# A two-layer fp32 encoder on one core: casts tied behind the last activation, operand sums by kind, residual loads tied to the stream

## The chip, the cores and the metric

The kernel runs on one core of one Trainium2 chip. The metric is the device time of one execution in microseconds (us). TensorE (PE) multiplies, ScalarE (ACT) casts and activates, VectorE (DVE) adds, subtracts and splits, GpSimd (POOL) and SyncE (SP) mostly start DMA transfers, each on a queue of its own: SP's is the hardware queue (q1), POOL's the software queue (q0).

## The reference

The encoder has two layers over 1024 tokens of width 1024, each with a mixer and a gated feed-forward part, with a layer norm behind each sum:

```python
for layer in range(DEPTH):                      # DEPTH = 2
    y = even_mixer(...) if layer % 2 == 0 else odd_mixer(...)
    x = layer_norm(DN_ALPHA * x + y, mix_ln_g[layer], mix_ln_b[layer])
    x = layer_norm(DN_ALPHA * x + swiglu(x, ffn_w_gate[layer], ffn_w_up[layer], ffn_w_down[layer]),
                   ffn_ln_g[layer], ffn_ln_b[layer])

def swiglu(x, w_gate, w_up, w_down):
    return (jax.nn.silu(x @ w_gate) * (x @ w_up)) @ w_down
```

The even mixer is latent attention with a Fourier branch, the odd one a gated unit whose spatial part mixes positions inside blocks of 128; each ends in an output projection. Everything is float32.

## The kernel before

An fp32 product is made of three matmuls. `split` makes of a tile a high part (ACT cast, line 135: `xoh`, `whi`) and a low part (DVE subtraction, line 136: `xol`, `wlo`), and `mm3` multiplies high by high (line 141), high by low (142) and low by high (143). So TensorE can't begin with a page before its cast, nor go past the first matmul before its subtraction.

After the even front (to about 557 us) the kernel is a row of stages: the output projection of the mixer (called mix), feed-forward part 0 (ffn0), the spatial part of the odd layer, its projection (odd), and feed-forward part 1 (ffn1). Each projection and each down-projection is a **reduce**.

A reduce works in seven products in place of eight (half-size blocks, with sums of blocks made before), in the order p = 1, 5, 6, 4, 7, 2, 3. A product runs over groups g of two page pairs. `load(p, g)` calls `stream`, which has SP fetch 512 KB of H (left pages, or their sums SA and SB) and 512 KB of W (right pages, or their sums TA and TB) into one of six `rx` tiles and splits them into one of six pairs of cells; a group is 24 matmuls of 128x512. The stage before has its last pages stored to memory by POOL, and the sums of the last page pairs (`page_sums`, lines 317 to 320) stored behind it, and the first groups of the next reduce (`lead`) are already loaded while it runs.

Besides, the reduce adds the residual: eight tiles of 512 KB, `xt[half, s]`, loaded by POOL (line 463), in all but the mix reduce multiplied by a gain and given a bias by `gained` (DVE, lines 469 and 470), then joined with the result from PSUM by `add` (line 457). The tiles come from pools that the stage before still uses, so a residual load waits for the tile's last reader. The two loads of the last mix page pair (`job`) and the stores of its sums go through POOL too.

The normalised rows are transposed and become operands of the following feed-forward part: besides four plain blocks, the sums S1 (made before) and, per slot s of four, S2, S4 and S3 (`all_sums`); each is a DVE subtraction (line 131) and a split. The feed-forward part's first two units, which run interleaved, take plain blocks first, then S2, S4 and S3. A unit ends in `emit`: a DVE addition (kept as `last_v`) and a Silu on ACT.

The order on each engine is made by a scheduler from the program's order, dependences and estimated readiness. `behind(marks)` adds an edge: an instruction is not put before the marked one on the same engine. `marks` are the instructions of the last `stream`: SP's DMA, ACT's cast, DVE's subtraction.

Of the kernel before, what the change touches and what calls it, by code (L numbers as in the profile page):

```python
# [112 lines left out]
class Trunk:  # L113
# [109 lines left out]
    def run(self):  # L223
        tc, nc, a = self.tc, self.nc, self.a
        with ExitStack() as top:
# [24 lines left out]
            self.vd = D_("vd", [P, NT, 256], 8)  # L250
            self.ahead = None
            with ExitStack() as fs:
# [156 lines left out]
    def reduce(self, st, resid, rgb, ln, keep, pre=None, left=()):  # L409
# [30 lines left out]
        def load(p, g):  # L440
            if (p, g) not in ops:
                ops[p, g] = self.stream(st, p, groups[g], raws, pairs)

# [16 lines left out]

        def residual(half):
            for s in range(4):
                nc.gpsimd.dma_start(xt[half, s], resid[token(half, s)])

# [44 lines left out]

        def sums(s):  # L510
            (a11, a12), (a21, s1) = kept[0, s], kept[1, s]
            self.sub(s1, s1, a11)
            self.split(*self.operand(self.S2, s), s1)
            self.sub(a12, a12, s1)
            self.split(*self.operand(self.S4, s), a12)
            self.sub(a21, a11, a21)
            self.split(*self.operand(self.S3, s), a21)

# [6 lines left out]
        def spread(jobs, k, of):  # L525
            i0, i1 = len(jobs) * k // of, len(jobs) * (k + 1) // of
            for j in jobs[i0:i1]:
                j()
        slots = range(4)
        for p in (1, 5, 6, 4, 7, 2):  # L530
            for g in range(n):
                load(p, g)
                if p == 1 and g == 1:
                    load(1, 2)
                    if rgb is not None:
                        rg, rb = (self.bcast(tmp(), a["ln_" + x][rgb[0], rgb[1]]) for x in "gb")
                    residual(0)
                    last = self.job(st, M - 1, True) if st is self.stage["mix"] else None
                if p == 5 and g == 0:
                    residual(1)  # L540
                if p == 6 and g == 0 and keep is None:
                    fg, fb = (self.bcast(self.raw_tile(), a["ln_" + x][ln[0], ln[1]]) for x in "gb")
                if p == 4 and g == 0 and pre is not None:
                    with self.behind(*self.marks):
                        pre()
                if p in (1, 5) and g > 1:
                    spread([lambda s=s: gained(p == 5, s) for s in slots], g - 2, n - 2)
                if p == 2:
                    spread([lambda s=s: normed1(s) for s in slots], g, n)
                for s in slots:  # L550
                    mm(p, g, s)
                    if p == 1 and s % 2 == 1 and left:
                        left.pop(0)()
                    if g == n - 1:
                        if p == 1:
                            add(0, s, lo, p, True)
                        elif p == 5:
                            add(0, s, hi, p, True)
                            add(1, s, hi, p, True)
                        elif p == 6:  # L560
                            add(0, s, hi, p)
                        elif p == 4:
                            add(1, s, lo, p, True, ALU.subtract)
                        elif p == 7:
                            add(1, s, lo, p)
                            add(1, s, hi, p)
                        else:
                            add(0, s, lo, p)
                            stat(0, s, 0)
# [20 lines left out]
        def all_sums():  # L590
            with self.behind(self.late):
                for s in slots:
                    sums(s)
        return [lambda q=q: turn0(q) for q in range(2)], all_sums
# [103 lines left out]
    def ffn(self, w0, weights, st, pend):  # L698
# [4 lines left out]
        def unit(j, w, tiles="yy"):  # L703
            sg = {}

            def emit(half, col, ps, sb, op):
                if col == 0:
                    self.last_v = nc.vector.tensor_tensor(sb, ps, sb, op=op).ins  # L708
                    nc.scalar.activation(sb, sb, AF.Silu)
                    sg[half] = sb  # L710
                    return
# [697 lines left out]
```

## Time and profile before

| | |
|---|---|
| median of 3 runs | 2541.53 us (2537.37 to 2542.77) |
| profiled execution | 2541.83 us |
| its span in the profile | 2540.0 us |
| PE busy | 2456.4 us, 97% |
| DVE busy | 1808.9 us, 71% |
| ACT busy | 1111.1 us, 44% |
| DMA | 170 GB/s over the span |

Busy time is the time in which an engine works on instructions, the span runs from the first to the last instruction, and the execution's time holds something around it. The profile's times in the text count from the start of the span. A row of busy time by stretches has the stretch, its length, then busy us (and instructions) of PE, its weight loads, DVE, ACT and POOL, then the granted clock, the DMA engines' busy share, and GB/s. A row in order of time has start, duration, engine, line, operation, output and inputs, and in brackets the idle time before and what ended it. A row of waits has who waited for whom, the total in us, how often, and the longest.

### The profile page before, as it was taken

Reading aid. Unit: us, or ns where it says so; the run is one execution under the profiler, and the core shown is the slowest. Engines: PE = TensorE matmul, PEld = TensorE weight load, DVE = VectorE, ACT = ScalarE, POOL = GpSimd, SP = SyncE. Lnnn points to the kernel's source line nnn. Section 1 sums busy time; section 2 is a strip of 40 time slices with the busy share of each in tenths; the row PEclk is TensorE's granted clock in tenths of the full one; section 3 lists DMA queues with packets and bytes.
Section 4 is the critical chain, followed back from the end, with each engine's and each line's share of the span. In section 5 each row is a group of like instructions: output and inputs, shape, how many; then the busy total and the mean of one; then the engine's idle time right before and its main releaser. Section 6 shows DMA issues by size and latency. Waiting matters only on the chain.

```text
span 2540.0 us, 33155 instructions
## 1 busy us (share of the span) xinstructions
PE 2456.4 (97%) x12294; PEld 2073.4 (82%) x12294; DVE 1808.9 (71%) x2537; ACT 1111.1 (44%) x1711; POOL 318.5 (13%) x527
## 2 busy tenths in 40 slices
PE   8989999998999999999999999988989999999997
PEld 6778888887878888887889998877878888887885
DVE  4348878767886776768678776768777676677667
ACT  3235555544553333333456446653463333333331
POOL 1000111010111111110002132430011111111001
PEclk9999999998999999999999999999999999999998
DMA  4122333138334444467654554667624444549553
GB/s 175 43 89 71 130 110 125 57 138 282 138 118 174 169 168 162 168 252 251 226 182 172 202 203 137 195 244 276 224 73 163 177 166 155 177 164 329 190 188 140
DMA packets 164329, 431.95 MB, mean 170 GB/s; under 512 B 20136, under 2 KB 26952, under 8 KB 164168
## 3 DMA queue, kind: packets, MB, share of 16 engines
q1 hardware_dynamic: 108216, 232.11, 27.8%
q0 software_dynamic: 55952, 197.73, 20.9%
q8 instruction: 96, 1.57, 0.2%
q14 instruction: 65, 0.53, 0.1%
HBM read 286.64 MB, written 138.41 MB: 167 GB/s over the span
## 4 chain that ended last, share of the span: by engine, by line
PE 81%; DVE 6%; issue 5%; DMA 4%; ACT 2%; POOL 1%; SPq 1%; DVEq 0%; ACTq 0%; POOLq 0%
PE b L142 18%; PE b L141 18%; PE b L143 18%; PE S L1316 6%; PE b L912 5%; PE mm L141 4%; PE mm L142 4%; PE mm L143 4%; PE mm L1335 2%; DVE xol L136 1%; DMA rx<-h 1%; PE b L848 1%; DMA x<-xs 1%; ACT xoh L135 1%; DVE st L475 1%
## 5 line engine op out<-in xcount | busy, mean ns | idle before, releaser
L135 ACT CAST whi<-raw 128x1024 fp32r<-128x1024 f32 (+3 forms) x277 | 261.2, 951 | 383.4 <-PE b L142 240.2
L135 ACT CAST xoh<-rx 128x1024 fp32r<-128x1024 f32 (+1 forms) x252 | 244.5, 1011 | 413.5 <-PE b L142 308.8
L141 PE MATMUL b<-xoh,whi 128*128 128x512 f32 x1040 | 410.7, 396 | 7.9 <-ACT xoh L135 7.9
L136 DVE TENSOR_TENSOR wlo<-raw,whi 128x1024 fp32r<-128x1024 f32 (+3 forms) x277 | 303.4, 1099 | 159.3 <-ACT whi L135 157.1
L142 PE MATMUL b<-xol,whi 128*128 128x512 f32 x1040 | 406.8, 391 | 0.0
L143 PE MATMUL b<-xoh,wlo 128*128 128x512 f32 x1040 | 406.4, 391 | 0.0
L136 DVE TENSOR_TENSOR xol<-rx,xoh 128x1024 fp32r<-128x1024 f32 (+1 forms) x252 | 287.6, 1168 | 166.0 <-ACT xoh L135 160.3
L142 PE MATMUL b<-xol,xoh 128*128 128x512 f32 x960 | 379.4, 395 | 22.3 <-DVE xol L136 22.3
L141 PE MATMUL b<-xoh 128*128 128x512 f32 x960 | 376.1, 394 | 8.5 <-ACT xoh L135 8.5
L143 PE MATMUL b<-xoh,xol 128*128 128x512 f32 x960 | 377.5, 393 | 0.0
L141 PEld LDWEIGHTS b<-xoh,whi 128*128 128x128 f32 x1040 | 196.6, 189 | 50.3 <-ACT xoh L135 8.8
L142 PEld LDWEIGHTS b<-xol,xoh 128*128 128x128 f32 x960 | 183.1, 191 | 63.3 <-DVE xol L136 25.5
L143 PEld LDWEIGHTS b<-xoh,wlo 128*128 128x128 f32 x1040 | 196.3, 189 | 41.3
L142 PEld LDWEIGHTS b<-xol,whi 128*128 128x128 f32 x1040 | 196.5, 189 | 40.4 <-issue 0.5
L141 PEld LDWEIGHTS b<-xoh 128*128 128x128 f32 x960 | 182.9, 190 | 47.6 <-ACT xoh L135 9.3
L143 PEld LDWEIGHTS b<-xoh,xol 128*128 128x128 f32 x960 | 183.1, 191 | 38.2
L663 ACT COPY y<-b 128x512 f32<-128x512 f32 x200 | 116.6, 585 | 192.7 <-PE b L143 186.1
L141 PE MATMUL b<-xah,whi 128*128 128x512 f32 x416 | 162.5, 391 | 1.3 <-ACT xah L135 1.3
L142 PE MATMUL b<-xal,whi 128*128 128x512 f32 x416 | 162.0, 389 | 0.0
L143 PE MATMUL b<-xah,wlo 128*128 128x512 f32 x416 | 161.9, 389 | 0.0
L131 DVE TENSOR_TENSOR raw<-raw,raw 128x512 f32<-128x512 f32 (+1 forms) x174 | 128.5, 739 | 28.2 <-DMA raw<-w_up 24.7
L708 DVE TENSOR_TENSOR y<-b,y 128x512 f32<-128x512 f32 x84 | 58.0, 690 | 82.9 <-PE b L143 82.6
(378 smaller groups left out, 4590.9 us busy)
## 6 DMA issues: line engine op xcount, KB each, us to landing
raw<-w_gate SPq DMA_DIRECT2D x44, 512.0 KB, 3.6
raw<-w_up SPq DMA_DIRECT2D x44, 512.0 KB
q<-w_down POOLq DMA_DIRECT2D x44, 512.0 KB, 5.3
h<-x POOLq DMA_DIRECT2D x44, 512.0 KB, 3.7
rx<-h SPq DMA_DIRECT2D x60, 256.0 KB, 3.0
rx<-w_down SPq DMA_DIRECT2D x60, 256.0 KB, 4.3
raw<-o_v SPq DMA_DIRECT2D x16, 512.0 KB, 6.1
x<-o_out POOLq DMA_DIRECT2D x16, 512.0 KB, 5.7
```

The source lines that it names most:

```text
L131: self.nc.vector.tensor_tensor(out, a, b, op=ALU.subtract)
L135: a = self.nc.scalar.copy(hi, src)
L136: return a.ins, self.nc.vector.tensor_tensor(lo, src, hi.bitcast(F32), op=ALU.subtract).ins
L141: mm(ps, lh, rh, start=start, stop=False, skip_group_check=skip)
L142: mm(ps, lh, rl, start=False, stop=False, skip_group_check=skip)
L143: mm(ps, ll, rh, start=False, stop=stop, skip_group_check=skip)
L475: nc.vector.bn_stats(stats[half, s][:, c, :], xt[half, s][:, c * 512:(c + 1) * 512])
L663: nc.scalar.copy(t, ps)
L708: self.last_v = nc.vector.tensor_tensor(sb, ps, sb, op=op).ins
L912: nc.tensor.matmul(ps[:, i * 256:(i + 1) * 256], l[:, b, k, c], r[:, k, :], start=start and k == 0 and i == 0 and m == 0, stop=k == 3 and ...
L1316: nc.tensor.matmul(sc[:, kb, :], l[:, s], r[:, kb * 512:(kb + 1) * 512], start=i == 0, stop=i == 4)
L1335: nc.tensor.transpose(ps[:, k, :], p[:, kt * P:(kt + 1) * P], self.ident)
```

## The change

Four edits, and no change in what is computed. Behind the first edited lines of the changed program line numbers are higher by up to nine.

1. `emit` also keeps the last Silu as `last_a` (the spatial part its last Gelu, by the same attribute). In a reduce, the casts and subtractions of product 1's groups that are not yet loaded are put behind `last_a` on ACT and `last_v` on DVE. In the mix reduce there is no such mark.
2. A residual tile is loaded by tile, not by half. Ahead of each load stands a memset of one column, and it is put behind the subtraction of the stream's last split. Half 0 goes with groups 1 and 2 of product 1, half 1 with product 1's last group and product 5's first.
3. The gains are spread to one group later for half 0, and from product 5's second group for half 1; the first `add` of half 0 goes from the end of product 1 to product 5's second group.
4. The sums are made by kind, four S2, four S4, four S3, and no longer slot by slot.

```diff
         def load(p, g):
             if (p, g) not in ops:
-                ops[p, g] = self.stream(st, p, groups[g], raws, pairs)
+                with self.behind(*((self.last_a, self.last_v) if p == 1 and self.last_a is not None else ())):
+                    ops[p, g] = self.stream(st, p, groups[g], raws, pairs)
...
-        def residual(half):
-            for s in range(4):
-                nc.gpsimd.dma_start(xt[half, s], resid[token(half, s)])
+        def residual(half, s):
+
+            with self.behind(self.marks[2]):
+                nc.vector.memset(xt[half, s][:, 0:1], 0.0)
+            nc.gpsimd.dma_start(xt[half, s], resid[token(half, s)])
...
-        def sums(s):
+        def sum_of(o, s):
             (a11, a12), (a21, s1) = kept[0, s], kept[1, s]
-            self.sub(s1, s1, a11)
-            self.split(*self.operand(self.S2, s), s1)
-            self.sub(a12, a12, s1)
-            self.split(*self.operand(self.S4, s), a12)
-            self.sub(a21, a11, a21)
-            self.split(*self.operand(self.S3, s), a21)
+            out, a, b = {self.S2: (s1, s1, a11), self.S4: (a12, a12, s1), self.S3: (a21, a11, a21)}[o]
+            self.sub(out, a, b)
+            self.split(*self.operand(o, s), out)
...
-                    residual(0)
                     last = self.job(st, M - 1, True) if st is self.stage["mix"] else None
-                if p == 5 and g == 0:
-                    residual(1)
+                if p == 1 and 0 < g < 3:
+                    for s in (2 * g - 2, 2 * g - 1):
+                        residual(0, s)
+                if (p == 1 and g == n - 1) or (p == 5 and g == 0):
+                    for s in (0, 1) if p == 1 else (2, 3):
+                        residual(1, s)
...
-                if p in (1, 5) and g > 1:
-                    spread([lambda s=s: gained(p == 5, s) for s in slots], g - 2, n - 2)
+                if p == 1 and g > 1:
+                    spread([lambda s=s: gained(0, s) for s in slots], g - 2, n - 1)
+                if p == 5 and g == 0:
+                    spread([lambda s=s: gained(0, s) for s in slots], n - 2, n - 1)
+                if p == 5 and g > 0:
+                    spread([lambda s=s: gained(1, s) for s in slots], g - 1, n - 1)
+                if (p, g) == (5, 1):
+                    for s in slots:
+                        add(0, s, lo, 1, True)
...
-                for s in slots:
-                    sums(s)
+                for o in (self.S2, self.S4, self.S3):
+                    for s in slots:
+                        sum_of(o, s)
...
                     self.last_v = nc.vector.tensor_tensor(sb, ps, sb, op=op).ins
-                    nc.scalar.activation(sb, sb, AF.Silu)
+                    self.last_a = nc.scalar.activation(sb, sb, AF.Silu).ins
```

Three places of the instruction order follow.

TensorE in the mix reduce, where product 5's last groups and product 6's first meet, of before (`b_5626` to `b_5647` are the banks of product 6, `b_5738` to `b_5752` those of product 5's third group, `xoh` and `xol` the split pages):

```order
L141 MATMUL b_5626<-xoh 128x512
L141 MATMUL b_5738<-xoh 128x512
L142 MATMUL b_5738<-xol,xoh 128x512
L141 MATMUL b_5745<-xoh 128x512
L142 MATMUL b_5745<-xol,xoh 128x512
```

and of the change, where the third group's banks are `b_5742` to `b_5756`:

```order
L142 MATMUL b_5640<-xol,xoh 128x512
L143 MATMUL b_5640<-xoh,xol 128x512
L141 MATMUL b_5647<-xoh 128x512
L141 MATMUL b_5742<-xoh 128x512
L142 MATMUL b_5742<-xol,xoh 128x512
L141 MATMUL b_5749<-xoh 128x512
```

Before, one matmul of product 6 stands ahead of product 5's third group; of the change 19 do (six for each of three banks, and one). On POOL's queue of the same place the loads of the page job (`raw<-mix`) moved ahead of all eight residual loads, and the stores of its sums, which stood behind them before as well, are now issued directly behind them, while the loads themselves are later.

VectorE at the start of ffn0's reduce, of before (`rx` tiles are the stream's pages, lines 317 to 320 the last page sums, `gb` gain or bias):

```order
L317 TENSOR_TENSOR x_9736<-x_9550,x_9715 128x512
L318 TENSOR_TENSOR x_9735<-x_9550 128x512
L319 TENSOR_TENSOR x_9735<-x_9736,x_9550 128x512
L469 TENSOR_TENSOR q_9756<-q_9756,gb_9785 128x1024
L320 TENSOR_TENSOR x_9736<-x_9715,x_9735 128x512
L470 TENSOR_TENSOR q_9756<-q_9756,gb_9787 128x1024
L469 TENSOR_TENSOR x_9755<-x_9755,gb_9785 128x1024
L136 TENSOR_TENSOR xol<-rx_9879,xoh 128x1024
L470 TENSOR_TENSOR x_9755<-x_9755,gb_9787 128x1024
L136 TENSOR_TENSOR xol<-rx_9884,xoh 128x1024
```

and of the change:

```order
L320 TENSOR_TENSOR x_9744<-x_9723,x_9743 128x512
L136 TENSOR_TENSOR xol<-rx_9788,xoh 128x1024
L465 MEMSET x_9763 128x1
L465 MEMSET q_9764 128x1
L465 MEMSET q_9765 128x1
L465 MEMSET y_9766 128x1
L136 TENSOR_TENSOR xol<-rx_9853,xoh 128x1024
L136 TENSOR_TENSOR xol<-rx_9858,xoh 128x1024
L136 TENSOR_TENSOR xol<-rx_9889,xoh 128x1024
L136 TENSOR_TENSOR xol<-rx_9894,xoh 128x1024
L472 TENSOR_TENSOR x_9763<-x_9763,gb_9793 128x1024
L472 TENSOR_TENSOR q_9764<-q_9764,gb_9793 128x1024
```

The four memsets come behind the third group's splits, and the splits of two more groups stand between them and the first gain, which before stood ahead of the third group's. On POOL's queue the last page and its two sums moved ahead of the residual loads. ffn1's reduce reads the same.

VectorE at the end of the operand sums of ffn0 (S2, S4 and S3 formed at line 131 and split at line 136; `q_6677` is the last slot's S4), of before:

```order
L131 TENSOR_TENSOR q_6677<-q_6677,x_6479 128x4x128
L131 TENSOR_TENSOR x_6479<-q_6676,x_6479 128x512
L136 TENSOR_TENSOR wlo_6782<-raw_5993,whi_6781 128x1024
L136 TENSOR_TENSOR xol<-q_6677,xoh 128x4x128
L136 TENSOR_TENSOR xol<-x_6479,xoh 128x4x128
```

and of the change, where it is `q_6685`:

```order
L131 TENSOR_TENSOR q_6685<-q_6685,x_6487 128x4x128
L131 TENSOR_TENSOR y_6415<-x_6621,y_6415 128x512
L131 TENSOR_TENSOR x_6439<-x_6621,x_6439 128x512
L136 TENSOR_TENSOR xol<-q_6685,xoh 128x4x128
L136 TENSOR_TENSOR xol<-y_6415,xoh 128x4x128
L136 TENSOR_TENSOR xol<-x_6439,xoh 128x4x128
L131 TENSOR_TENSOR x_6463<-q_6684,x_6463 128x512
L131 TENSOR_TENSOR x_6487<-q_6684,x_6487 128x512
L136 TENSOR_TENSOR wlo_6790<-raw_6001,whi_6789 128x1024
L136 TENSOR_TENSOR xol<-x_6463,xoh 128x4x128
L136 TENSOR_TENSOR xol<-x_6487,xoh 128x4x128
```

Of the 24 instructions of the sums three stand behind the last S4's subtraction before, and nine of the change.

In the odd part, all of the last spatial unit's ACT work and its normalising additions on VectorE now stand ahead of the casts and splits of the odd reduce's third group. In F's place, where that reduce goes from product 1 to product 5, lines 317 to 320 of its last page sums and gains still stand between the pages' splits; the adds of half 0 now stand behind the splits.

## Rows read from the trace of the kernel before

**Rows 1.** The page, part 1: busy time of each engine, share, instructions.
```profile
PE 2456.4 (97%) x12294; PEld 2073.4 (82%) x12294; DVE 1808.9 (71%) x2537; ACT 1111.1 (44%) x1711; POOL 318.5 (13%) x527
```

**Rows 2.** Waits of TensorE, whole span.
```profile
PE b L142 <- DVE xol L136: 22.3, 8, 6.6
...
PE b L141 <- ACT xoh L135: 16.4, 4, 5.0
...
PE b L848 <- ACT whi L839: 8.9, 1, 8.9
```

**Rows 3.** Busy time by stretches of 16 us: eight borders, then two undisturbed ones.
```profile
564.00:580.00 16.00, 12.01 (x42) 9.04 (x41) 4.27 (x4) 4.72 (x5) 2.40 (x5) 0.79 1.04 400
590.00:606.00 16.00, 11.04 (x40) 8.62 (x39) 8.51 (x11) 3.63 (x4) 0.00 (x0) 0.79 0.81 270
714.00:730.00 16.00, 12.26 (x42) 9.20 (x41) 15.90 (x25) 9.44 (x16) 0.00 (x0) 0.79 0.11 34
1138.00:1154.00 16.00, 10.33 (x37) 8.02 (x36) 11.36 (x12) 3.33 (x4) 1.93 (x4) 0.79 1.01 382
1690.00:1706.00 16.00, 7.07 (x29) 5.77 (x28) 8.19 (x10) 9.99 (x19) 2.55 (x4) 0.68 1.04 390
1726.00:1742.00 16.00, 9.45 (x36) 7.38 (x35) 15.90 (x18) 2.37 (x3) 2.14 (x4) 0.79 0.74 269
1896.00:1912.00 16.00, 11.81 (x40) 8.79 (x39) 15.04 (x23) 8.57 (x15) 0.00 (x0) 0.79 0.10 33
2320.00:2336.00 16.00, 10.82 (x39) 8.41 (x38) 12.63 (x12) 3.34 (x5) 1.59 (x3) 0.79 1.02 394
610.00:626.00 16.00, 16.00 (x73) 13.23 (x72) 14.31 (x17) 9.39 (x10) 0.00 (x0) 1.00 0.70 236
740.00:756.00 16.00, 16.00 (x72) 13.27 (x71) 12.72 (x19) 6.54 (x9) 2.13 (x4) 1.00 0.46 165
```

**Rows 4.** Busy time by stretches, ffn0's reduce, a short stall.
```profile
1223.00:1226.00 3.00, 2.06 (x10) 1.38 (x9) 3.00 (x4) 1.83 (x2) 0.00 (x0) 1.00 0.72 210
```

**Rows 5.** Waits of all engines, 564 to 575 us, start of the mix reduce.
```profile
ACT xoh L135 <- DMA rx<-mix: 9.8, 1, 9.8
...
PE b L141 <- ACT xoh L135: 3.5, 1, 3.5
```

**Rows 6.** DMA, 1133 to 1143 us: packets, MB, share by queue; issues, us to landing.
```profile
q0 software_dynamic: 783, 2.87, 70.5%
q1 hardware_dynamic: 701, 1.27, 33.0%
...
x<-xs POOLq DMA_DIRECT2D x3, 512.0 KB, 9.3
```

**Rows 7.** Waits of all engines, 1138 to 1150 us, start of ffn0's reduce.
```profile
PE b L142 <- DVE xol L136: 5.7, 1, 5.7
DVE x L469 <- DMA x<-xs: 4.6, 1, 4.6
```

**Rows 8.** VectorE in order of time, 1700 to 1740 us.
```profile
1721.81 1.22 DVE L469 TENSOR_TENSOR q<-q,gb 128x1024 f32<-128x1024 f32 x1
...
1726.10 0.69 DVE L317 TENSOR_TENSOR x<-x,x 128x512 f32<-128x512 f32 x1 [1.93 <-DMA tp<-x]
...
1734.30 5.77 DVE L136 TENSOR_TENSOR xol<-rx,xoh 128x1024 fp32r<-128x1024 f32 x5
```

**Rows 9.** Groups of instructions by line, VectorE: busy us, mean ns, idle before.
```profile
L1322 DVE RECIPROCAL den<-den 128x1 f32<-128x1 f32 x64 | 10.4, 162 | 16.9 <-ACT p L1321 16.5
```

**Rows 10.** Waits of all engines, 1686 to 1706 us, start of the odd reduce.
```profile
ACT xoh L135 <- DMA rx<-tp: 7.9, 2, 6.4
```

**Rows 11.** VectorE in order of time, 706 to 724 us, the sums of ffn0.
```profile
708.70 0.69 DVE L131 TENSOR_TENSOR y<-y,x 128x512 f32<-128x512 f32 x1
...
720.75 0.68 DVE L131 TENSOR_TENSOR q<-q,x 128x512 f32<-128x512 f32 x1
```

**Rows 12.** Waits of TensorE, 714 to 724 us, start of ffn0.
```profile
PE b L141 <- ACT xoh L135: 3.7, 1, 3.7
```

More of the change, by code (lines that the diff above doesn't have):

```diff
@@ L250, in run @@
             self.vd = D_("vd", [P, NT, 256], 8)
-            self.ahead = None
+            self.ahead = self.last_a = None
             with ExitStack() as fs:
@@ L554, in reduce @@
                     if g == n - 1:
-                        if p == 1:
-                            add(0, s, lo, p, True)
-                        elif p == 5:
+                        if p == 5:
                             add(0, s, hi, p, True)
@@ L566, in reduce @@
                             add(1, s, hi, p)
-                        else:
+                        elif p == 2:
                             add(0, s, lo, p)
```

## The prediction

> **What bounds the kernel now.** I read the page first, then the waits of each engine, then busy time by stretches, then the waits and the order of time at the places that stood out. The span is 2540.0 us, and TensorE is busy for 97% of it, VectorE for 71% [rows 1], so an edit pays only where it takes idle time or half-clock time from TensorE. The profiled execution took 2541.83 us: 1.8 us lie outside the span, and the median of the three runs shown is 2541.53, so I add and subtract from 2541.8 and treat it as the median.
>
> TensorE's waits are few: 22.3 us for the low halves of the left pages in eight waits, 16.4 us for the high halves in four, 8.9 us once for a weight split of the spatial stage [rows 2]. Each is at a border between two stages. An idle stretch is not all it costs: the granted clock falls to 1.2 GHz behind it. The reader sees it best by counting matmuls in 16 us: undisturbed stretches hold 73 and 72, at clock 1.00, so one costs 16 / 72.5 = 0.221 us; a group of 24 takes 5.3 us. The eight stretches at borders hold 42, 40, 42, 37, 29, 36, 40 and 39, at clocks of 0.68 to 0.79 [rows 3]. The loss of each is 16 minus its count times 0.221:
>
> A, start of the mix reduce, 6.7 us; B, its product 5, 7.2; C, start of ffn0, 6.7; D, start of ffn0's reduce, 7.8; E, start of the odd reduce, 9.6; F, its product 5, 8.1; G, start of ffn1, 7.2; H, start of ffn1's reduce, 7.4. Together 60.7 us. That is all the change can take away.
>
> A short stall has no such tail: from 1223 to 1226 us TensorE is idle for 0.94 us, and the clock stays 1.00 [rows 4].
>
> **The change part by part.**
>
> *Residual loads tied to the stream's splits.* In A the cast of the stream waits 9.8 us for `rx<-mix` and TensorE 3.5 us for the cast [rows 5], while eight 512 KB residual loads are on POOL's queue. Behind, they are released by splits of the second and third group; the page job's own two loads go first. The stream then meets an empty software queue. I take the whole 6.7 us; the low bound is half of it, 3.4, if the loads of the first release still share with the third group's pages.
>
> B is the reload of the last page sums, `mixSB`. Two things move. 19 matmuls of product 6 now stand ahead of product 5's third group: 19 x 0.221 = 4.2 us of cover against the 5.0 us stall [rows 2]. Against it, the two stores of the sums now stand behind all eight residual loads on POOL's queue: 4.2 MB, which at the software queue's 287 GB/s (2.87 MB in 10 us [rows 6]) is 14.6 us from the release. With A gone TensorE arrives earlier too. I leave 2.0 us of stall, too short for a clock tail [rows 4], and gain 5.2; bounds 0 and 7.2.
>
> D and H are one form. TensorE waits 5.7 us for `xol`, and VectorE stood 4.6 us before it at line 469, the gain of a residual tile that was still on its way; the pages' splits are queued behind it on VectorE [rows 7]. A residual load took 9.3 us to land there [rows 6]. After the change the four splits of the next two groups stand ahead of the first gain, and the last page and its sums are stored ahead of the residuals. What is late next is the stream: while the software queue is full, the hardware queue moved 1.27 MB in 10 us, 127 GB/s [rows 6], and a group needs 1.05 MB in 5.3 us, 198 GB/s. The queue holds the last page, two sums and four residual tiles, 7 x 0.524 = 3.67 MB, 12.8 us at 287 GB/s. In that time TensorE uses 2.4 groups and the stream brings 1.55: 0.85 of a group, 4.5 us, less what the six raw tiles hold in advance, which I put at 1.5 us. So 3.0 us stay, in pieces too short for the clock to fall. Gains 4.8 and 4.4; bounds 0, and the full 7.8 and 7.4.
>
> A rule speaks against my 3.0 us, and the rest does not need it. The Trainium skill (DMA: Bandwidth & Descriptors, section "Queues, rings and completion order") says that a DMA engine takes turns between the queues that have work, packet by packet. If equal turns meant equal bytes, the stream would get half of 414 GB/s, 207, above its need, D and H would lose nothing, and the sum would be 6 us lower, some 2490. The packets are indeed almost even (783 to 701), but the bytes are 2.87 to 1.27 MB [rows 6], so I go by the bytes.
>
> In F VectorE has 13 instructions between the two splits of a group, from 1721.81 to 1734.30, among them five passes of residual gains, four adds and a 1.9 us wait for `tp<-x` [rows 8]. After, the most that stands between two groups are four passes, three sums of 0.6 us and two memsets, without the adds. A pass takes 1.14 us by its rate there (12.5 us, less the wait and eight sums and adds of 0.6, leaves 5.8 for five). With the same wait that is 4.6 + 1.8 + 1.9 = 8.3 us in place of 12.5. The stall of 6.6 us [rows 2] shrinks by 4.2 to 2.4; with a little clock tail I leave 3.0. Gain 5.1; bounds 0 and 8.1.
>
> The memsets are 32 VectorE instructions of one column. The nearest row is a reciprocal of 128x1, 162 ns [rows 9]: 5.2 us in all, bounds 0 and 5.2 on VectorE, which is idle for over a quarter of the span. I take nothing on TensorE's path. Their danger is not length but waiting: one that meets a tile still being stored holds up the splits behind it (a rival below).
>
> *Casts behind the last activation.* This matters most in E. The normalisation of the last spatial unit waits behind casts of the new stage's pages on ScalarE, and these wait 7.9 us for `rx<-tp` [rows 10]; TensorE waits 8.9 us at line 848 [rows 2]. After, all of that unit's ScalarE work stands ahead of those casts, and nothing that TensorE needs first hangs on DMA. What is late next is the first page's own cast and low half. I leave 1.0 and gain 8.6; bounds 5.0 (the pages of the next groups are then late instead) and 9.6. In D and H it lets the last Silu, the last page and its sums go some 3 us earlier, which is in the figures above.
>
> *Sums by kind.* In C the 24 instructions of the sums run from 708.70; twenty of them are done when the last S4, whose cast TensorE waits for, is formed at 720.75 [rows 11], so one takes 0.60 us. Formed at 721.4 and cast by about 721.9, it ends a wait of 3.7 us [rows 12], so TensorE arrived at 718.2. In the new order nine of the 24 stand behind it instead of three, so it is formed six steps earlier, at 717.8, and cast by 718.3; its low half is the third instruction behind, done at 719.5. Against 718.2 that leaves 1.3 us, without a clock tail. Gain 5.4 in C, and by the same order 5.9 in G; low bounds 3.0 each, since the other operands are then formed later, upper bounds the losses.
>
> **Sum.** 6.7 + 5.2 + 5.4 + 4.8 + 8.6 + 5.1 + 5.9 + 4.4 = 46.1 us; 2541.8 - 46.1 = 2495.7, say 2496. All low bounds: 3.4 + 0 + 3 + 0 + 5 + 0 + 3 + 0 = 14.4, 2527. All upper bounds: 2481.
>
> **Rivals.**
>
> *All goes*: no stall of over a microsecond stays at the eight borders, 2481. For it: undisturbed stretches use 0.46 and 0.70 of the DMA [rows 3]. Against: the bytes to be moved near each border are the same.
>
> *Half is given back*: the software queue and VectorE's order put new waits in B, D, F and H as large as the old. Only A, C, E and G pay: 6.7 + 5.4 + 8.6 + 5.9 = 26.6, 2515. For it: in D's stretch the DMA is full already (share 1.01 [rows 3]), and F's gains still stand ahead of its pages.
>
> *Slower*: the tied loads land after VectorE has reached the gains. The loads of half 0 have two groups, 10.6 us, and those of half 1 one group, 5.3 us, of cover. If the software queue holds 11 tiles (page, two sums, eight residuals), 5.77 MB, the first release lands after 20.1 us: a wait of 9.5 us; half 1 lands after 9.3 us: 4.0. Each brings a clock tail of about 2.1 us (7.8 lost in D for 5.7 waited [rows 3, 7]): 17.7 us in each of three reduces, 53 in place of 23.3, against the 26.6 won, and B's stall longer by about 5: 2550. It decides from a landing of some 20 us, twice what the row shows, at all three places.
>
> *Nothing*: the stalls only move to the next group, where the same bytes are still short: within 5 us of 2541.
>
> **How the numbers follow.** I give my sum 0.58 (own range 2487 to 2508), all goes 0.11, half given back 0.20, nothing 0.05, slower 0.06. A change within 0.2%, 5 us, is about what this kernel's runs can't tell from none. The first three cases are faster by more: 0.89; same 0.05, slower 0.06. The range takes the sum, nearly all of the best case and most of the half case: 2480 to 2524.
>
> **What would show it.** Right: the granted clock stays 1.00 at the starts of both feed-forward stages and of the mix and odd reduces, the normalising matmul of line 848 (857 then) no longer waits 8.9 us, and the counts at those borders rise to 66 or more in 16 us. D and H right: several waits under 2 us in place of one over 5. Wrong: a VectorE memset or gain that waits over 5 us for a DMA, `rx` landing times of 8 us or more behind the release, or half-clock stretches one or two groups later than before.

## The result, and the profile after

The change takes 2513.59 us (median of 4 runs, 2511.52 to 2516.69) against 2539.69 before (4 runs, 2537.37 to 2542.77): a ratio of 0.9897, 95% interval 0.988 to 0.9915, 26.1 us faster. It lies in the forecast range, 17.6 us above the forecast time, and 1.4 us from the 2515 worked out for the rival "half is given back".

TensorE's waits in the profile of the change, over the whole span, beside [rows 2]:

```profile
PE b L142 <- DVE xol L136: 17.5, 10, 4.9
PE b L141 <- ACT xoh L135: 8.2, 4, 3.9
...
PE b L857 <- ACT xoh L135: 2.2, 1, 2.2
```

The waits for high halves are halved and that of 8.9 us at the normalising matmul is 2.2. The waits for low halves are ten in place of eight, and only 4.8 us less. Where they are is seen by counting matmuls again, as in [rows 3]; a border now comes earlier by what was won ahead of it. Busy time by stretches, the change:

```profile
564.00:580.00 16.00, 16.00 (x72) 13.28 (x71) 10.85 (x20) 6.49 (x7) 5.84 (x12) 1.00 1.03 375
580.00:606.00 26.00, 18.96 (x67) 14.49 (x67) 10.84 (x12) 6.00 (x6) 0.07 (x1) 0.87 0.94 363
709.00:725.00 16.00, 15.23 (x67) 12.02 (x66) 16.00 (x27) 11.61 (x19) 0.00 (x0) 1.00 0.12 34
1122.00:1138.00 16.00, 16.00 (x73) 13.24 (x72) 10.49 (x10) 6.40 (x7) 1.64 (x4) 1.00 1.03 404
...
1706.00:1722.00 16.00, 11.07 (x40) 8.66 (x39) 15.55 (x19) 3.10 (x4) 2.15 (x4) 0.79 0.91 317
...
1738.00:1754.00 16.00, 12.05 (x43) 9.75 (x44) 10.80 (x11) 3.03 (x4) 0.00 (x0) 0.79 0.73 251
1881.00:1897.00 16.00, 14.77 (x64) 11.71 (x63) 15.93 (x26) 10.36 (x19) 0.54 (x1) 1.00 0.12 33
2299.00:2315.00 16.00, 14.16 (x61) 11.05 (x60) 13.41 (x18) 6.20 (x7) 2.09 (x4) 1.00 0.80 289
```

C, D, G and H rise to 67, 73, 64 and 61 at clock 1.00. The mix reduce and the odd reduce still hold slow stretches, at other moments than before, so for these a longer stretch has to be counted. Of the kernel before:

```profile
564.00:606.00 42.00, 32.58 (x121) 25.24 (x120) 22.79 (x27) 12.99 (x13) 4.55 (x9) 0.84 0.89 317
...
1600.00:1766.00 166.00, 150.52 (x726) 126.12 (x725) 127.47 (x167) 84.03 (x147) 46.93 (x75) 0.95 0.68 231
```

and the odd reduce of the change, the same work:

```profile
1584.00:1750.00 166.00, 151.13 (x719) 125.50 (x718) 126.78 (x174) 83.26 (x147) 46.88 (x75) 0.96 0.69 234
```

At 0.221 us a matmul:

| place | counts, before and after | won, us | forecast |
|---|---|---|---|
| A and B, mix reduce | 121 and 139 (72 + 67) | 4.0 | 11.9 |
| C, start of ffn0 | 42 and 67 | 5.5 | 5.4 |
| D, ffn0's reduce | 37 and 73 | 7.9 | 4.8 |
| E and F, odd reduce | 726 and 719 | -1.5 | 13.7 |
| G, start of ffn1 | 40 and 64 | 5.3 | 5.9 |
| H, ffn1's reduce | 39 and 61 | 4.9 | 4.4 |

The sum is 26.1 us, as is the difference of the medians; the spans of the two profiled executions differ by 27.5. The first row hides two things: A gives 6.6 us (42 and 72), and B's stretch from 580 to 606 us loses 2.7 against before (79 and 67). The row of E and F hides as much: laid beside each other by the number of the matmul, the change gets 10.6 us further ahead of the kernel before across E, and falls back by 12.6 until the end of F's product. H's count is that of one execution: three of the kernels below, which leave that stage as it is, hold 72, 70 and 72 there, so some 2 us of H vary without an edit. What was forecast and did not come lies in two stages.

In the odd reduce VectorE's order of time shows what took the place of the old waits (start, duration, instruction, idle time before):

```profile
1683.19 0.69 DVE L317 TENSOR_TENSOR x<-x,x 128x512 f32<-128x512 f32 x1 [4.96 <-DMA tp<-x]
...
1701.50 1.23 DVE L472 TENSOR_TENSOR x<-x,gb 128x1024 f32<-128x1024 f32 x1 [4.92 <-DMA x<-xs]
...
1739.54 6.90 DVE L136 TENSOR_TENSOR xol<-rx,xoh 128x1024 fp32r<-128x1024 f32 x6
```

and TensorE's waits for low halves in the same 166 us:

```profile
PE b L142 <- DVE xol L136: 11.7, 3, 4.9
```

VectorE waits 5.0 us for a store of a page that the page sums will overwrite, then 4.9 us for a residual tile, each time with splits behind. From then on it is idle twice for under 0.5 us and, from 1716 to 1742 us, not at all: it is busy for all 26.00 us (shown with the experiment on that). Yet TensorE waits 4.7 us for the splits that begin at 1739.54.

In the mix reduce the DMA is full. Queues and issues from 575 to 590 us (packets, MB, share; us from issue to landing):

```profile
q0 software_dynamic: 1138, 4.14, 67.9%
q1 hardware_dynamic: 1133, 2.06, 35.7%
rx<-mixTB SPq DMA_DIRECT2D x4, 256.0 KB, 9.3
...
x<-x POOLq DMA_DIRECT2D x1, 512.0 KB, 14.8
...
mixSB<-raw POOLq DMA_DIRECT2D x1, 512.0 KB, 13.8
```

The stream gets 2.06 MB in 15 us, 137 GB/s, and the store of the sums lands 13.8 us after its issue.

### The profile page after: what moved, and what is told of

It reads as the page before. It is cut to its first block, busy times and chain, and to the rows that moved or that the text cites. A ratio compares the mean times of both kernels' runs of the same rounds, so it can differ in the third digit from the quotient of the medians.

```text
span 2512.5 us, 33168 instructions
## 1 busy us (share of the span) xinstructions
PE 2446.8 (97%) x12294; PEld 2066.2 (82%) x12294; DVE 1809.2 (72%) x2569; ACT 1111.2 (44%) x1711; POOL 317.2 (13%) x527
## 4 chain that ended last, share of the span: by engine, by line
PE 85%; issue 5%; DVE 4%; DMA 2%; ACT 2%; SPq 1%; POOL 0%; DVEq 0%; POOLq 0%; ACTq 0%
PE b L142 19%; PE b L143 19%; PE b L141 19%; PE S L1325 6%; PE b L921 6%; PE mm L141 4%; PE mm L142 4%; PE mm L143 4%; PE mm L1344 2%; DVE xol L136 1%; PE b L857 1%; DMA rx<-w_down 1%; ACT q L378 0%; DMA gb<-ln_b 0%; ACT xoh L135 0%
```

## The experiments

Medians are of four runs (ten in one case named there). The kernel before stood at 2539.5 to 2541.5 us beside each of them, so a difference of 2 us between two of these kernels says little by the medians; there the traces are laid beside each other by the number of the matmul.

### Undoing one part

**Sums slot by slot again.**

```diff
-                for o in (self.S2, self.S4, self.S3):
-                    for s in slots:
+                for s in slots:
+                    for o in (self.S2, self.S4, self.S3):
                         sum_of(o, s)
```

> The change with its sums made slot by slot again. If the order of the sums alone won the starts of ffn0 and ffn1 (5.6 us each where the traces are laid beside each other), both waits of about 4 us and their half-clock stretches return, the time is some 11 us above the change, about 2525, and every other border keeps the time of the change. Rival: the earlier start of the stage, by the other edits, had taken part of these waits; then they come back to less than half, under 5 us in all, about 2518.

2523.24 us, 9.7 above the change. TensorE's waits at ffn0's start (700 to 735 us) and at ffn1's (1875 to 1900 us):

```profile
PE b L141 <- ACT xoh L135: 3.7, 1, 3.7
...
PE b L141 <- ACT xoh L135: 4.2, 1, 4.2
```

They are back, as long as before. The order of the sums alone won C and G.

**Casts not tied to the last activation.**

```diff
-                with self.behind(*((self.last_a, self.last_v) if p == 1 and self.last_a is not None else ())):
-                    ops[p, g] = self.stream(st, p, groups[g], raws, pairs)
+                ops[p, g] = self.stream(st, p, groups[g], raws, pairs)
```

> The change without the tie of product 1's groups to the last activation and addition. Theory: the tie won only the start of the odd reduce (up to 10 us there), and the starts of both feed-forward reduces (7.9 and 5 us won) hang on the gains standing behind the splits; then only the odd reduce's start is slower and the time is 2514 to 2524. Rival: the tie, by letting the last page and its sums leave earlier, is what won the feed-forward reduces; then both of their waits of over 5 us return and the time is 2525 to 2537.

2519.16 us, 5.6 above the change; the waits of over 5 us in the feed-forward reduces do not return. TensorE's waits in the odd stage:

```profile
PE b L856 <- ACT whi L847: 8.5, 1, 8.5
PE b L142 <- DVE xol L136: 6.9, 2, 3.6
```

The old wait of 8.5 us is back, and the waits for low halves are 6.9 us where the change has 11.7. So the tie does take away the old wait, and of the 6.3 us of waiting that it saves there 4.8 come back behind it. By the number of the matmul this kernel is 7.0 us later than the change behind that wait and 2.7 later at the end of the odd reduce's product 5. Another 2.5 us lie in ffn0's reduce, with two waits of 1.1 and 0.9 us; two kernels below that keep the tie lose 2.2 and 2.3 there, so they are not shown to be the tie's.

**Residual loads, gains and adds as before.** The places of `gained` and of the first `add` are those of the kernel before, too.

```diff
-        def residual(half, s):
-
-            with self.behind(self.marks[2]):
-                nc.vector.memset(xt[half, s][:, 0:1], 0.0)
-            nc.gpsimd.dma_start(xt[half, s], resid[token(half, s)])
+        def residual(half):
+            for s in range(4):
+                nc.gpsimd.dma_start(xt[half, s], resid[token(half, s)])
```

> The change with residual loads, gains and adds as they were: what is left are the tie of the casts and the order of the sums. Theory: the waits at the feed-forward reduces' starts return (13 us), the mix reduce's start is late again (about 4 us net), and the odd reduce is no worse than in the change, since its three new waits come from the moved gains and loads: about 2525 to 2532. Rival: the tie alone is enough for the feed-forward reduces; then about 2512 to 2518, and with the odd reduce better even below.

2534.43 us (ten runs, 2531.03 to 2535.83), 20.8 above the change and 2.4 above the range expected. Waits from 1120 to 1147 us, ffn0's reduce:

```profile
POOL x L464 <- DMA h<-x: 8.4, 1, 8.4
DVE x L470 <- DMA x<-xs: 8.2, 1, 8.2
...
PE b L142 <- DVE xol L136: 6.1, 1, 6.1
```

D and H are back, the theory's reading of them holds so far, and the tie alone is not enough. The odd reduce is no better than in the change: three waits for low halves of 10.5 us and one of 3.7. The same total in another place was the first sign that something other than a single wait holds it.

**Loads tied, gains as before.** Only the places of `gained` and of the first `add` are undone.

```diff
-                if p == 1 and g > 1:
-                    spread([lambda s=s: gained(0, s) for s in slots], g - 2, n - 1)
...
+                if p in (1, 5) and g > 1:
+                    spread([lambda s=s: gained(p == 5, s) for s in slots], g - 2, n - 2)
```

> The change with tied residual loads, but gains and first adds in their places of before, one group earlier for half 0 and one later for half 1. Theory: with the loads tied, the gains now stand before tiles that have not landed, VectorE waits 5 us or more with the pages' splits behind it, in both feed-forward reduces: 8 to 16 us above the change, 2522 to 2530, and the odd reduce's middle also worse. Rival: the place of the loads is all that counts and the gains find their tiles anyway: within 4 us of the change, with the odd reduce's end of product 5 less crowded.

2515.52 us, 1.9 above the change, which their intervals (0.9891 to 0.992, and 0.988 to 0.9915) can't tell from none: the theory fell and the rival holds. In ffn0's reduce VectorE waits for no residual tile, with the gains where they were; TensorE's only wait there is 1.8 us. It is the loads' place that won D and H. POOL's order of time of the change shows how:

```profile
1116.71 0.53 POOL L731 DMA_DIRECT2D h<-x  x1 [5.16 <-DVE x L725]
1118.64 0.53 POOL L348 DMA_DIRECT2D ffn0SA<-x  x1 [1.40 <-DVE x L319]
...
1121.54 0.53 POOL L466 DMA_DIRECT2D x<-xs  x1 [0.63 <-DVE y L465]
```

and that of the kernel with the residual as before:

```profile
1123.53 0.53 POOL L464 DMA_DIRECT2D q<-xs  x1 [7.44 <-DMA ffn0TA<-q]
...
1136.62 0.53 POOL L464 DMA_DIRECT2D x<-xs  x1 [8.40 <-DMA h<-x]
```

There POOL itself stands for 7.4 us before the first residual load, whose tile is still being stored, with the last page and both sums behind it. With a memset ahead of each load, POOL reaches the loads only behind the splits, and the page and its sums leave first. No run moves the loads without the memsets, so what each of the two gives is not shown. In the odd reduce of the kernel with the gains as before, one wait of 11.1 us and one of 2.0 stand where the change has three with 11.7: again about the same total.

### What holds the odd reduce

**Sums later.** The last two pairs of page sums are formed one to two groups later.

```diff
-            return [lambda: mixed(29), lambda: (summed(6, self.marks[2]), mixed(30)), lambda: mixed(31), lambda: summed(7, self.marks[2])]
+            return [lambda: mixed(29), lambda: mixed(30), lambda: mixed(31), lambda: summed(6, self.marks[2]), lambda: None, lambda: None, lambda: None, lambda: summed(7, self.marks[2])]
```

> The change with the odd reduce's last two pairs of page sums one to two groups later, so that VectorE does not wait 5.0 us for a store of tp ahead of the spatial part's last products. Theory: from the last unit to the end of product 5 VectorE's own work is the bound of the odd reduce (26.00 of 26 us busy in the last stretch), so the waits at its start go (2.3 and 2.2 us) and come back at the end of product 5: within 2.5 us of the change. Rival: the wait for the store is the cause, and some 5 to 7 us are won.

2513.64 us, the time of the change. Its waits for low halves are five with 11.6 us in place of three with 11.7, and in the same 166 us it does as many matmuls:

```profile
1584.00:1750.00 166.00, 153.27 (x719) 126.16 (x718) 126.80 (x174) 83.42 (x146) 46.84 (x75) 0.96 0.70 236
```

The wait for the store was not the cause.

**Half 1's gains in product 6.** Product 5's results stay in their banks until product 4 begins, so the odd reduce's half-1 gains and first adds can wait one product.

```diff
-                if p == 5 and g > 0:
+                if p == 5 and g > 0 and n != 4:
                     spread([lambda s=s: gained(1, s) for s in slots], g - 1, n - 1)
+                if p == 6 and n == 4:
+                    gained(1, g)
+                    add(1, g, hi, 5, True)
...
-                            add(1, s, hi, p, True)
+                            if n != 4:
+                                add(1, s, hi, p, True)
```

> The change with the odd reduce's half-1 gains, and the first adds that follow each, moved from product 5 to product 6: 9 us of gains and 5 us of adds or so leave the stretch in which VectorE is full. Theory: the last wait of 4.9 us and its half-clock stretch go, 6 to 8 us below the change, 2505 to 2508, and product 6 shows no new wait. Rival: the odd reduce is held by the DMA (share 0.93 from 1683 to 1716 us), and what is won at product 5 is lost again there: within 2.5 us.

2502.09 us (2499.82 to 2504.68), ratio to the kernel before 0.9846 (0.9827 to 0.9865), 11.5 below the change and more than expected. Not all of it is the edit's. The same work in 166 us, and the stretch around product 5:

```profile
1582.00:1748.00 166.00, 158.78 (x759) 132.11 (x758) 129.66 (x175) 86.55 (x149) 46.50 (x75) 0.98 0.74 255
1716.00:1742.00 26.00, 26.00 (x115) 21.33 (x114) 25.46 (x28) 10.02 (x10) 0.00 (x0) 1.00 0.83 281
```

against the change:

```profile
1716.00:1742.00 26.00, 20.32 (x89) 16.20 (x87) 26.00 (x30) 8.01 (x8) 0.36 (x1) 0.96 0.52 176
```

759 matmuls in place of 719 are 8.8 us; the rest lies in stages that the edit leaves as they are (the mix reduce holds 76 matmuls from 580 to 606 us in place of 67, and H 72 in place of 61). From 1716 to 1742 us TensorE is busy throughout, with the DMA at 0.83 where it had 0.52: not the DMA, but VectorE's work was the bound. VectorE is almost as busy there as in the change (25.46 of 26 us); what differs is that more of it is splits of pages, first in the change, then with the gains later:

```profile
L136 DVE TENSOR_TENSOR xol<-rx,xoh 128x1024 fp32r<-128x1024 f32 x9 | 10.6, 1220 | 0.0
...
L136 DVE TENSOR_TENSOR xol<-rx,xoh 128x1024 fp32r<-128x1024 f32 x12 | 14.2, 1216 | 0.0
```

No run moved work off VectorE in another way.

**Half 0's gains later as well.** On top of the last, half 0's gains and first adds stand in product 5, one tile a group.

```diff
+                if p == 5 and n == 4:
+                    gained(0, g)
+                    add(0, g, lo, 1, True)
```

> The kernel with the odd reduce's half-1 gains in product 6 (2502.1), with its half-0 gains, and the first adds behind them, spread over product 5, one tile a group, instead of product 1 and product 5's start. Theory: the wait of 4.9 us for a residual tile that has not landed, with the pages' splits behind it, goes with its 4.2 us on TensorE and the half-clock stretch: 2496 to 2499; the wait for the store of tp at the start (2.7 us) stays. Rival: the stretch is held by the stream on the DMA, 2500 to 2503.

2505.41 us: above both ranges, and not faster than the 2502.09 it was to beat (ratios 0.9853 to 0.9883, and 0.9827 to 0.9865). The wait of 4.0 us did go, but two of about 2 us stand in product 5 and 6 in its place (waits for low halves five with 5.6 us, against two with 4.6). By the number of the matmul the two kernels' odd reduces differ by 0.3 us; the rest of the 3.3 us lies ahead of them (1.3 in the mix reduce, 2.3 in ffn0's), in stages that are the same in both.

### What holds the mix reduce

**No residual there.** The eight loads are left out and the tiles set to zero by GpSimd.

```diff
+                if st is self.stage["mix"]:
+                    nc.gpsimd.memset(xt[half, s], 0.0)
+                    return
```

> The change without the mix reduce's residual: its eight loads are left out and the tiles are set to zero by the idle GpSimd, so that the first layer norm sees the projection alone. It prices the whole meeting of the residual loads with the stream and the last sums. Theory: with the software queue empty the stream gets its 198 GB/s, the sums' reload is early, and the 6.3 us of waits at 585 to 600 us with their half-clock stretch fall to under 1.5: 6 to 9 us below the change, 2505 to 2508. Rival: the sums themselves are late (formed at 574 to 579 us, stored and loaded again), so that 3 to 5 us stay, as they did with half 0's loads alone: 2509 to 2512.

2504.66 us, 8.9 below the change: the theory holds. TensorE's wait for high halves is 1.3 us in place of 6.3, and the stretch holds 99 matmuls for 67:

```profile
580.00:606.00 26.00, 24.19 (x99) 19.22 (x98) 18.36 (x21) 9.91 (x10) 0.00 (x0) 0.93 0.76 261
```

and the store of the last sums, which took 13.8 us to land, takes 4.9:

```profile
mixSB<-raw POOLq DMA_DIRECT2D x1, 512.0 KB, 4.9
```

At 0.221 us a matmul the 26 us would hold 118, so the change loses 11.2 us there, and the meeting of the residual with the stream and that store is 7.1 of them. 4.1 stay: behind waits of 1.3 and 0.5 us the granted clock still fell to 0.50, which is 1.2 GHz:

```profile
590.00:593.00 3.00, 3.00 (x8) 2.35 (x8) 1.72 (x3) 0.00 (x0) 0.00 (x0) 0.50 0.94 313
```

**Half 1's loads at product 5's last group** and their first adds in product 6, mix reduce alone.

```diff
+                if st is self.stage["mix"]:
+                    if (p, g) == (5, n - 1):
+                        for s in slots:
+                            residual(1, s)
-                if (p == 1 and g == n - 1) or (p == 5 and g == 0):
+                elif (p == 1 and g == n - 1) or (p == 5 and g == 0):
```

> The change with the mix reduce's half-1 residual loads tied to product 5's last group, behind the stores of the last sums, and their first adds moved to product 6; every other stage as in the change. Theory: in the change eight loads and two stores, 5.2 MB in one row on the software queue, hold the stream to some 137 GB/s for 17 us and make the reload of the sums late; with half of them behind the stores the waits of 2.5, 1.0 and 4.1 us at 585 to 600 us shrink to under 3 in all and the half-clock stretch goes: 4 to 7 us below the change, 2507 to 2510. Rival: the stream is late because its own pages come in one burst there (the start of the stage), then under 2 us.

2513.35 us, the time of the change; the theory's sum did not come. One wait of 7.0 us stands for two. ScalarE's cast, POOL's loads and SP's reload in order of time:

```profile
592.48 2.94 ACT L135 CAST xoh<-rx 128x1024 fp32r<-128x1024 f32 x3 [5.48 <-DMA rx<-mixSB]
```

```profile
584.75 2.18 POOL L466 DMA_DIRECT2D x<-x  x4 [4.83 <-DVE x L465]
```

```profile
586.41 0.32 SPq L396 DMA_DIRECT2D rx<-mixSB  x1
```

The four loads start 1.7 us ahead of the very reload that TensorE waits for, which then takes 6.0 us. Fewer loads ahead of the store, and as many beside the reload. The stretch from 580 to 606 us holds 76 matmuls for 67, but so does a kernel with these loads in their old place (the one with half 1's gains later).

**All three edits together** (sums later, half 1's gains in product 6, half 1's loads at product 5's last group).

> All three edits together. If they work on waits of their own, the sum: theory 2513.6 less 5 for the mix reduce and 7 to 12 for the odd one (with room on VectorE, the later sums now pay as well), 2496 to 2502. Rival: the odd reduce is held by something that all of them share, then no better than the best of the three alone.

2504.87 us: not the sum, and no better than the gains' edit alone (2502.09). The odd reduce holds 744 matmuls in its 166 us, against 759 without the later sums: they cost 15 matmuls there, or 3.3 us.

**Half 1's loads at product 6's second group**, with the odd reduce's half-1 gains in product 6.

```diff
-                    if (p, g) == (5, n - 1):
+                    if (p, g) == (6, 1):
```

> The kernel with the odd reduce's half-1 gains in product 6 (2502.1), and the mix reduce's half-1 loads tied to product 6's second group, behind the reload of the last sums, which they met when they were tied to product 5's last group. Theory: the reload, which then took 6 us beside them, takes 3, the wait of 7.2 us (or 6 to 7 in three pieces) shrinks to 2 to 4, and 3 to 6 us are won against 2502: 2496 to 2499. Rival: the four loads of half 0 and the late sums are enough to hold the stream up; then within 2 us of 2502.

2502.24 us, as without it: the rival, by the total time. The place itself holds 85 matmuls in the stretch, for 76 in the kernel it is compared with, and one wait of 4.8 us:

```profile
587.87 2.94 ACT L135 CAST xoh<-rx 128x1024 fp32r<-128x1024 f32 x3 [2.85 <-DMA rx<-mixSB]
```

The kernel compared with had itself 9 matmuls more there than the change (waits of 3.1, 1.6 and 0.8 us), with the same mix reduce, so the place varies from kernel to kernel by as much as the edit gives.

**The sums first, too.** The last mix sums are formed behind product 1's third group in place of product 5's first, with the last edit and half 0's later gains in the odd reduce.

```diff
-                if (p, g) == (5, 0) and last is not None:
+                if (p, g) == (1, 1) and last is not None:
                     last(self.marks[2])
```

> Both edits of the last two, and the mix reduce's last sums formed behind product 1's third group instead of product 5's first, some 4 us earlier, with their stores between the residual loads. If the late store of the sums is what is left of the mix reduce's wait, the time is the sum of the two gains and 2 us more, 2489 to 2494; if the stream's rate beside half 0's loads is, then the sum of the two alone, 2491 to 2497.

2500.34 us (2498.12 to 2502.24), ratio to the kernel before 0.9849 (0.9832 to 0.9865): above both ranges, and the lowest median, but its interval is that of the odd gains' edit (0.9846). One wait of 3.6 us stays in the mix reduce, with 90 matmuls in the stretch. Three of half 0's loads are still issued ahead of the store of `mixSB`, which lands 8.6 us after its issue; without any loads it was 4.9, and the wait 1.3. No run takes half 0's loads away alone.

## Why the prediction was right, and where it was not

The time lies in the range, but the sum was 46.1 us and 26.1 came. Of that shortfall of 20.0 the time shows 17.6, as the sum started from 2541.8 and the median before is 2539.69. That the rival's 2515 lies so near is luck: it let A, C, E and G pay and B, D, F and H not, but D and H paid, E's gain was lost again, and B got worse.

*C and G.* Right in mechanism and size (5.4 and 5.9 forecast, 5.5 and 5.3 found; 9.7 for both by undoing them).

*D and H.* Right that they would go, the size too small for D (4.8, found 7.9; the 3.0 us left for a starved stream did not come), about right for H. In the profiles of four of the experiments waits of 0.6 to 1.9 us do stand in ffn0's reduce and cost 2.2 to 2.5 us, so 3.0 was the top of what came. The reason given was half wrong. The splits standing ahead of the gains do not matter: with the gains put back the loss stays away. What the loads' place changes is that POOL no longer waits for a tile under store with the last page behind it. The step "the last page and its sums are stored ahead of the residuals" carried it.

*E.* Right that the 8.9 us wait goes and that the tie is what takes it (10.6 us won at the border); wrong that 8.6 us would stay won. What was written beside its low bound, that the next groups would be late instead, is what came, and took all of it.

*F.* The step that failed: the stall was read as 13 instructions between two splits, and shortened by those that moved away. VectorE's work until the end of product 5 was not summed. The change takes nothing out of it: half 1's gains go from product 5's last two groups to its last three, and half 0's last two gains and its four first adds come into product 5 from product 1. So the forecast 5.1 us, and E's 8.6 with it, turned into -1.5; the run that moved half 1's gains and adds out of product 5 won 8.8 there. The rival "half is given back" named F's gains ahead of its pages, and was right there; it was wrong on D and H.

*A and B.* A went as said: 72 matmuls, clock 1.00. B is the second failed step: a gain of 5.2 was forecast, and 2.7 were lost. The eight loads' 14.6 us on the software queue were written down (the store landed after 13.8), the price of the late store was put at 2.0 us, and the stream's 127 GB/s, which D's term used against a need of 198, was left out of B. The two together cost 7.1 us in that stretch by leaving out the loads, and no run prices them one by one. D was given the shortage that B had.

*The memsets* cost 1.4 us on VectorE in all, at 0.06 us each, in place of the 5.2 put down, and VectorE is never idle ahead of one. A nearer row than the reciprocal stood in the trace of the kernel before:

```profile
L1057 DVE MEMSET fo<- 128x1 f32 x4 | 0.1, 59 | 0.0
```

The "slower" rival's wait for a tile that has not landed came in one reduce of three, at 4.9 us.

*The clock term.* Stalls left at 2 us and under were said to have no tail, by one row of 0.94 us. In ffn0's and ffn1's starts and D and H the clock stayed 1.00, but no wait there is longer than 1.1 us. Stalls of 4.7 and 4.9 us brought 0.79 over 16 us, as in [rows 3]. In between it does not hold: the clock was 0.50 from 590 to 593 us behind a wait of 2.4 us in the change, and behind waits of 1.3 and 0.5 us without the residual, and it fell behind one of 1.9 us with the sums later:

```profile
1719.50:1722.50 3.00, 3.00 (x8) 2.31 (x7) 3.00 (x5) 0.00 (x0) 0.00 (x0) 0.50 0.91 337
```

So B's 2.0 us, had they come, might have had a tail too.

*The signs.* Two of the three that were named for "wrong" came: `rx` landing times over 8 us (9.3 in the mix reduce), and half-clock stretches later than before, in the mix and odd reduces. They pointed at the two steps that failed, though the time lay in the range.

## What to carry to other kernels

Before counting a wait as won, add up the work that the in-order engine behind it has to do until the next point that all must reach: where that fills the stretch (26.00 of 26 us here), removing one wait only moves it. Look then for work whose result is not needed until later, and move it past that point; that gave 8.8 us in this stage, where removing or moving waits changed it by under 3. The engine's busy share does not tell the two apart (25.46 of 26 us after); what it works on first does. And a bulk load put on another queue is not out of the way: the question is what else the DMA carries in those microseconds, and whether a store that somebody waits for stands behind it.

## What the runs showed of the hardware

A VectorE memset of 128x1 took 0.06 us, and several are recorded as starting 0.01 us behind the start of a longer instruction:

```profile
1692.94 0.75 DVE L858 SCALAR_TENSOR_TENSOR wlo<-b,og,q 128x512 f32<-128x512 f32 x1
1692.95 0.06 DVE L465 MEMSET x<- 128x1 f32 x1
```

So a view of waits can name a memset where the engine was held by the splits around it: of TensorE's wait of 11.1 us with the gains as before it names line 465. With both queues full, packets were shared almost evenly again (1138 to 1133) and the bytes two to one (4.14 to 2.06 MB), as in [rows 6]: by the Trainium skill (DMA: Bandwidth & Descriptors, section "Queues, rings and completion order") a DMA engine takes turns between queues packet by packet. The profile's counts are even, as that would have it, and its packets are 3.6 and 1.8 KB on average, so the bytes are not; whether the profile's packets are those that the Trainium skill means, which hold several descriptors each, no run shows. Two waits of 2.2 and 2.0 us some 4 us apart, at 1684 and 1690 us, left the granted clock at 1.00, where one of 2.6 us at 1682 with half 1's gains later brought 0.50, so the length of a wait alone does not settle it (the change first):

```profile
1683.00:1699.00 16.00, 11.73 (x59) 9.54 (x59) 13.32 (x20) 7.50 (x8) 4.82 (x9) 1.00 0.93 333
...
1685.00:1688.00 3.00, 3.00 (x11) 2.08 (x9) 3.00 (x4) 1.99 (x2) 1.08 (x2) 0.50 0.94 371
```
